# A hybrid decoder layer on one core: the output projection as seven block products per 1024 tokens

## The chip, the core and the metric

One Trainium2 chip; the program runs on one of its cores. TensorE (PE) multiplies, VectorE (DVE), ScalarE (ACT) and GpSimd (POOL) do the rest, SyncE (SP) issues the DMAs. Each engine works through its own queue in order and waits on semaphores of the others. The metric is the device time of one execution in microseconds (us); three executions of the kernel before took 2698.26 to 2699.79 us, median 2699.1.

## The reference, cut to what matters

One layer over 4096 tokens of width 1024. One input projection gives the inputs of three head groups and a gate; the branch outputs, 2048 wide together, are gated and go through one output projection, a residual add and a final norm.

```python
h = rms_norm(x, norm_g[l])
proj = h @ w_in[l]
u_lru, q_gla, k_gla, v_gla, g_lr, q_xa, gate = jnp.split(proj, split_points, axis=-1)
...                      # y_lru, y_gla, y_xa: recurrence, linear attention, cross-attention
y = jnp.concatenate([y_lru, y_gla, y_xa], axis=-1) * jax.nn.silu(gate)
x = x + y @ w_out[l]     # (4096 x 2048) @ (2048 x 1024)
...
return rms_norm(x, final_norm_g)
```

Every product of the projections is computed from operands split in two: a high part (fp32r, a rounded copy) and a low part (operand minus high part). A product is then three matmuls, high x high, high x low and low x high (`mm3`).

## The kernel before

The tokens are taken in four blocks of 1024 (BLK), each of two units of 512 (UNIT). The first stage loops over blocks, and in a block over 17 head groups, written out in `orders`: L0 to L7 (recurrence), X0 to X3 (cross-attention), V, G, Q (linear attention). For each group and unit TensorE multiplies the group's weights (whi, wlo) with the normed input (hh, hl); generators that `tick()` moves on do the rest on the other engines. Weights come through two raw buffers (L109) and are split by ScalarE (L110) and VectorE (L111). Each group's gated output, 128 channels over a block, is stored to a DRAM tile y_d (`store_y`, L297). The inputs hh, hl of a unit take 16 KB per partition each, in pool hp, two of each.

The last stage is the output projection, in 32 steps of 128 tokens. `load_y` (L754 to L763) loads the 2048 channels of 128 tokens as yr, splits them into yh (L759) and yl (L760) and loads x. `out_mm` gives, for each of the 16 channel tiles ct and the two halves n of the 1024 outputs, three matmuls of a 128 x 128 stationary piece of y and 512 columns of the weights: 96 per 128 tokens into two PSUM banks. `finish` adds the residual (L776), squares (L778), takes the root on GpSimd (`rstd_of`, L68 and L70), scales (L782, the last step L787) and stores (L783, L789). All of w_out stays in SBUF as high and low parts, split once (`wo_split`, L701 to L706): the first four channel tiles during the last head groups by `wo_gen`, into hp buffers that the first unit has left, the other twelve at the start of the stage.

What sets the order: the program is written in one order, and a scheduler then orders each engine's queue by priorities and its own estimate of time, so that instructions of neighbouring parts mix. Buffers of a pool are waited for by semaphores. PSUM has two pools of four banks, acc and aux. All DMAs go through SP's queue, in the order in which they stand there.

## Time and profile before

| | |
|---|---|
| median of three runs | 2699.1 us |
| the profiled execution: time, and its span | 2699.65 us, 2697.9 us |
| TensorE busy | 2660.9 us, 13338 matmuls |
| VectorE, ScalarE, GpSimd busy | 1381.3, 1156.6, 92.4 us |
| granted TensorE clock, mean | 0.999 |
| DMA | 231.64 MB, mean 86 GB/s |

The span is counted from the first to the last instruction that the profile shows. Matmuls are pipelined: each is drawn some 389 ns long (for 512 columns) but the next one starts while it runs, so start times give the rate and busy sums don't. In a timeline a row has its start, its length, the engine, the line of the kernel, the operation with the tile written and the tiles read, and in brackets how long the engine had been idle before and who ended that.

### The profile page before, as it was taken

The page shows a single profiled execution, that of the slowest core. Times are in us where ns is not written, and L with a number is a line of the kernel's source. Part 1 is how long each engine was busy: PE and PEld are TensorE (multiplying, and loading weights), DVE is VectorE, ACT ScalarE, POOL GpSimd, SP SyncE. Part 2 cuts the span into 40 slices and gives each one's busy share as a digit, 9 for nine tenths or more (in the row PEclk, how much of TensorE's full clock was granted, in tenths as well). Part 3 has the DMA queues.
Part 4 walks back from the last instruction along what each step waited for, and adds up shares of the span by engine and source line. Part 5 has one row for each costly group of instructions (what it writes and reads, how often), then busy time and mean ns, then how long its engine had stood idle before and what let it go on. Part 6 is the DMA issues. An engine that isn't in the chain of part 4 may idle for free.

```text
span 2697.9 us, 32855 instructions
## 1 busy us (share of the span) xinstructions
PE 2660.9 (99%) x13338; PEld 2249.6 (83%) x13338; DVE 1381.3 (51%) x2349; ACT 1156.6 (43%) x1802; POOL 92.4 (3%) x197
## 2 busy tenths in 40 slices
PE   7999999999999999999999999999999999999998
PEld 6888888888888888888887888888878888888887
DVE  6466546656664666567456757645673222222221
ACT  6355535653654465356436636643572111111110
POOL 3000000000000000000000000000000000000000
PEclk9999999999999999999999999999999999999999
DMA  8211112431212133112213312111253222222221
GB/s 276 67 59 57 63 59 71 127 99 57 67 55 75 49 119 120 58 57 65 65 49 105 116 38 82 59 61 51 65 187 131 96 102 94 94 94 94 94 94 63
DMA packets 119928, 231.64 MB, mean 86 GB/s; under 512 B 6528, under 2 KB 73184, under 8 KB 115680
## 3 DMA queue, kind: packets, MB, share of 16 engines
q1 hardware_dynamic: 119776, 229.54, 26.2%
q8 instruction: 104, 1.70, 0.3%
q14 instruction: 48, 0.39, 0.0%
HBM read 179.19 MB, written 50.33 MB: 85 GB/s over the span
## 4 chain that ended last, share of the span: by engine, by line
PE 86%; DMA 4%; DVE 4%; ACT 4%; issue 1%; POOL 1%; SPq 0%; DVEq 0%; POOLq 0%; ACTq 0%
PE out L75 8%; PE out L74 8%; PE out L76 8%; PE gate L74 7%; PE gate L75 7%; PE gate L76 7%; PE u L75 4%; PE u L76 4%; PE u L74 4%; PE q L75 3%; PE q L74 3%; PE q L76 3%; DMA x<-in_x 2%; PE vp L477 2%; PE vp L476 2%; PE vp L475 2%
## 5 line engine op out<-in xcount | busy, mean ns | idle before, releaser
L74 PE MATMUL gate<-hh,whi 128*128 128x512 f32 x1024 | 400.6, 391 | 0.0
L75 PE MATMUL out<-wolo,yh 128*128 128x512 f32 x1024 | 398.8, 389 | 0.8 <-DVE wolo L706 0.6
L76 PE MATMUL gate<-hh,wlo 128*128 128x512 f32 x1024 | 398.8, 389 | 0.0
L74 PE MATMUL out<-wohi,yh 128*128 128x512 f32 x1024 | 398.0, 389 | 0.7 <-ACT wohi L705 0.7
L75 PE MATMUL gate<-hl,whi 128*128 128x512 f32 x1024 | 398.6, 389 | 0.0
L76 PE MATMUL out<-wohi,yl 128*128 128x512 f32 x1024 | 398.4, 389 | 0.0
L111 DVE TENSOR_TENSOR wlo<-raw,whi 128x1024 fp32r<-128x1024 f32 (+2 forms) x152 | 191.4, 1281 | 216.9 <-ACT whi L110 182.5
L776 DVE TENSOR_TENSOR xr<-xr,out 128x512 f32<-128x512 f32 x64 | 43.9, 687 | 444.7 <-PE out L76 444.7
L75 PEld LDWEIGHTS out<-wolo,yh 128*128 128x128 f32 x1024 | 192.2, 188 | 42.2 <-DVE wolo L706 2.1
L74 PEld LDWEIGHTS out<-wohi,yh 128*128 128x128 f32 x1024 | 192.1, 188 | 41.0 <-ACT wohi L705 1.1
L74 PEld LDWEIGHTS gate<-hh,whi 128*128 128x128 f32 x1024 | 192.3, 188 | 40.5 <-issue 1.5
L76 PEld LDWEIGHTS gate<-hh,wlo 128*128 128x128 f32 x1024 | 192.2, 188 | 40.3
L76 PEld LDWEIGHTS out<-wohi,yl 128*128 128x128 f32 x1024 | 192.2, 188 | 39.8
L110 ACT CAST whi<-raw 128x1024 fp32r<-128x1024 f32 (+2 forms) x152 | 162.4, 1095 | 146.5 <-PE gate L75 96.1
L75 PEld LDWEIGHTS gate<-hl,whi 128*128 128x128 f32 x1024 | 192.3, 188 | 39.1
L74 PE MATMUL u<-hh,whi 128*128 128x512 f32 x512 | 203.7, 398 | 0.0
L75 PE MATMUL u<-hl,whi 128*128 128x512 f32 x512 | 199.6, 390 | 0.0
L76 PE MATMUL u<-hh,wlo 128*128 128x512 f32 x512 | 199.4, 390 | 0.0
L333 DVE SCALAR_TENSOR_TENSOR uc<-u,prm_sb,uc 128x511 f32<-128x511 f32 (+2 forms) x192 | 142.9, 745 | 67.8 <-ACT uc L330 67.3
L759 ACT CAST yh<-yr 128x2048 fp32r<-128x2048 f32 x32 | 61.2, 1912 | 257.6 <-PE out L75 256.4
L778 ACT ACTIVATE j<-xr 128x512 bf16<-128x512 f32 x64 | 40.0, 625 | 304.9 <-DVE xr L776 304.9
L74 PE MATMUL q<-hh,whi 128*128 128x512 f32 x384 | 150.3, 391 | 0.0
(219 smaller groups left out, 4976.4 us busy)
## 6 DMA issues: line engine op xcount, KB each, us to landing
raw<-in_w_oth SPq DMA_DIRECT2D x72, 512.0 KB, 3.8
raw<-in_w_lru SPq DMA_DIRECT2D x64, 576.0 KB, 3.8
yr<-y_d SPq DMA_DIRECT2D x32, 1024.0 KB, 5.2
xt<-in_x_t SPq DMA_DIRECT2D x32, 512.0 KB, 3.8
y_d<-sg SPq DMA_DIRECT2D x32, 512.0 KB, 4.0
y_d<-i SPq DMA_DIRECT2D x32, 512.0 KB, 3.2
xr<-in_x SPq DMA_DIRECT2D x32, 512.0 KB, 3.4
out<-xr SPq DMA_DIRECT2D x31, 512.0 KB, 4.1
```

The costliest lines, as they stand in the source:

```text
L74: nc.tensor.matmul(o, w_hi, r_hi, start=start, stop=False)
L75: nc.tensor.matmul(o, w_hi, r_lo, start=False, stop=False)
L76: nc.tensor.matmul(o, w_lo, r_hi, start=False, stop=stop)
L110: nc.scalar.copy(out=hi[:, i, :width], in_=raw[:, :width])
L111: nc.vector.tensor_tensor(out=lo[:, i, :width], in0=raw[:, :width], in1=hi.bitcast(F32)[:, i, :width], op=ALU.subtract)
L333: nc.vector.scalar_tensor_tensor(out=uc[:, d:UNIT], in0=o[:, 0:UNIT - d], scalar=w, in1=uc[:, d:UNIT], op0=ALU.mult, op1=ALU.add)
L475: nc.tensor.matmul(o, hh, wh, start=kt == 0, stop=False)
L476: nc.tensor.matmul(o, hh, wl, start=False, stop=False)
L477: nc.tensor.matmul(o, hl, wh, start=False, stop=kt == KT - 1)
L759: nc.scalar.copy(out=yh, in_=yr)
L776: nc.vector.tensor_tensor(out=xt[:, c], in0=xt[:, c], in1=o[n], op=ALU.add)
L778: nc.scalar.activation(out=junk, in_=xt[:, c], func=AF.Square, accum_out=ss[:, n:n + 1])
```

## The change

The output projection of a block is seen as a product of 2 x 2 blocks: w_out's 2048 x 1024 as A11, A12, A21, A22, and y's 2048 channels x 1024 tokens as B11, B12, B21, B22 (the first index is the half of the channels, the second the unit of 512 tokens). Instead of eight products of blocks it computes seven, P1 to P7, of sums and differences of blocks (Strassen's method in Winograd's form), and adds them up into the two halves of the outputs for both units.

`wout_gen`, started in the second block after its third entry, loads w_out, scales the GLA rows, makes the four sums S1 to S4 of weight blocks on VectorE and stores them, with A12 and A22, to DRAM tiles ws_d; it runs between the head groups. In the last stage nothing of w_out stays in SBUF: for each product the weights are loaded anew (`w_load`), 512 KB per step of two channel tiles, into three buffers wraw, and split into wh and wl. A product has four steps of 24 matmuls. `prep_hi` of a step is issued three steps ahead (the cast of the token side, th, and of the weights, wh), `prep_lo` two steps ahead (tl, wl). The y blocks of 2 MB each are loaded in two pieces into the four hp buffers, which the first stage now names h0 to h3; the sums of token blocks are made in place before P5 and P4. The four banks of a product are copied or added to x rows by `evac`: after P7 come the norms of the eight pieces of 128 tokens (`out_norm`), three pieces of work per step. In the last product of all, TensorE takes the four row blocks one after the other, each with its eight channel tiles, and each row block's end follows at once. y_d is laid out as 16 tiles of 128 channels x 1024 tokens.

```diff
-    y_ds = [dram.tile([NSUB, P, 16, P], F32, name=f"y_d{b}", tag=f"y_d{b}") for b in range(nblk)]
+    y_ds = [dram.tile([16, P, BLK], F32, name=f"y_d{b}", tag=f"y_d{b}") for b in range(nblk)]
+    ws_ds = [dram.tile([P, 6, 512], F32, name=f"ws_d{c}", tag=f"ws_d{c}") for c in range(8)]
...
-        hh = hp.tile([P, KT, UNIT], F32R, tag="hh", name="hh")
-        hl = hp.tile([P, KT, UNIT], F32R, tag="hl", name="hl")
+        k = hslot[0] % 2
+        hslot[0] += 1
+        hh = hp.tile([P, KT, UNIT], F32R, tag=f"h{2 * k}", name="hh")
+        hl = hp.tile([P, KT, UNIT], F32R, tag=f"h{2 * k + 1}", name="hl")
...
-        nc.sync.dma_start(out=y_ds[b][:, :, ct, :].rearrange("s p t -> p s t"),
-                          in_=y.rearrange("p (s t) -> p s t", t=P))
+        nc.sync.dma_start(out=y_ds[b][ct], in_=y)
...
+    def wout_gen():
+        for c in range(8):
+            r0 = wp.tile([P, LW], F32, tag="raw", name="raw")[:, :D]
+            r1 = wp.tile([P, LW], F32, tag="raw", name="raw")[:, :D]
+            nc.sync.dma_start(out=r0, in_=w_out[c * P:(c + 1) * P, :])
+            nc.sync.dma_start(out=r1, in_=w_out[(c + 8) * P:(c + 9) * P, :])
+            yield 1
+            yield 1
+            if c < 4:
+                nc.scalar.activation(out=r1, in_=r1, func=AF.Copy, scale=hgn[:, c:c + 1])
+            a11, a21, a12, a22 = r0[:, :512], r0[:, 512:], r1[:, :512], r1[:, 512:]
+            s1 = wk.tile([P, UNIT], F32, tag="t2", name="s1")
+            s2 = wk.tile([P, UNIT], F32, tag="t2", name="s2")
+            nc.vector.tensor_tensor(out=s1, in0=a21, in1=a22, op=ALU.add)
+            nc.vector.tensor_tensor(out=a21, in0=a11, in1=a21, op=ALU.subtract)
+            nc.vector.tensor_tensor(out=s2, in0=s1, in1=a11, op=ALU.subtract)
+            nc.vector.tensor_tensor(out=a11, in0=a12, in1=s2, op=ALU.subtract)
+            d = ws_ds[c]
+            nc.sync.dma_start(out=d[:, 0:2, :], in_=r0.rearrange("p (a n) -> p a n", a=2))
+            nc.sync.dma_start(out=d[:, 2:4, :], in_=r1.rearrange("p (a n) -> p a n", a=2))
+            nc.sync.dma_start(out=d[:, 4, :], in_=s1)
+            nc.sync.dma_start(out=d[:, 5, :], in_=s2)
...
-                if last and u == 0:
-                    spawn(pending[0] if b + 1 < nblk else wo_gen(range(0, 4)))
+                if last and u == 0 and b + 1 < nblk:
+                    spawn(pending[0])
+            if b == 1 and ei == 2:
+                spawn(wout_gen())
...
+    tsp = ctx.enter_context(tc.tile_pool(name="tsp", bufs=4))
+    wrp = ctx.enter_context(tc.tile_pool(name="wrp", bufs=3))
+    wsp = ctx.enter_context(tc.tile_pool(name="wsp", bufs=4))
+    rp = ctx.enter_context(tc.tile_pool(name="rp", bufs=1))
+    fg_b = rp.tile([P, D], F32, name="fg_b")
+    CH = 2
+    NCH = 8 // CH
+    SEQ = [("P1", None, "acc", True), ("P5", S1, "aux", True), ("P2", A12, "acc", False),
+           ("P3", S4, "aux", False), ("P6", S2, "acc", True), ("P4", A22, "aux", True),
+           ("P7", S3, "acc", False)]
+    steps = [(b, p, c) for b in range(nblk) for p in range(len(SEQ)) for c in range(NCH)]
+    B, R = {}, {}
+    place = {"B11": 2, "B22": 3, "B12": 0, "B21": 1}
+    def load_b(b, n):
+        rows = slice(0, 8) if n[1] == "1" else slice(8, 16)
+        u = int(n[2]) - 1
+        if b > 0:
+            if n == "B11":
+                place["B11"], place["B22"] = place["B22"], place["B11"]
+        t = hp.tile([P, 8, UNIT], F32, tag=f"h{place[n]}", name=n)
+        src = y_ds[b][rows, :, usl(u)].rearrange("c p t -> p c t")
+        for i in range(2):
+            nc.sync.dma_start(out=t[:, 4 * i:4 * i + 4], in_=src[:, 4 * i:4 * i + 4])
+        B[b, n] = t
...
+    T, W = {}, {}
+    def w_load(q):
+        if q >= len(steps):
+            return
+        b, p, c = steps[q]
+        raw = wrp.tile([P, CH, 512], F32, tag="wraw", name="wraw")
+        for i in range(CH):
+            ct = c * CH + i
+            slot = SEQ[p][1]
+            nc.sync.dma_start(out=raw[:, i], in_=w_out[ct * P:(ct + 1) * P, 0:512] if slot is None
+                              else ws_ds[ct][:, slot, :])
+        W[q] = raw
+    def prep_hi(q):
+        if q >= len(steps):
+            return
+        b, p, c = steps[q]
+        cs = slice(c * CH, (c + 1) * CH)
+        n = SEQ[p][0]
+        if n == "P1":
+            if c == 0 and b == 0:
+                for nm in ("B11", "B22", "B12", "B21"):
+                    load_b(b, nm)
+            t = B[b, "B11"][:, cs]
+        elif n == "P5":
+            b11, b12, b22 = (B[b, m][:, cs] for m in ("B11", "B12", "B22"))
+            t = tsp.tile([P, CH, 512], F32, tag="t1", name="t1", bufs=2)
+            nc.vector.tensor_tensor(out=t, in0=b12, in1=b11, op=ALU.subtract)
+            nc.vector.tensor_tensor(out=b12, in0=b22, in1=b12, op=ALU.subtract)
+            nc.vector.tensor_tensor(out=b11, in0=b22, in1=t, op=ALU.subtract)
+        elif n == "P2":
+            t = B[b, "B21"][:, cs]
+        elif n == "P3":
+            t = B[b, "B22"][:, cs]
+        elif n == "P6":
+            t = B[b, "B11"][:, cs]
+        elif n == "P4":
+            t = B[b, "B21"][:, cs]
+            nc.vector.tensor_tensor(out=t, in0=B[b, "B11"][:, cs], in1=t, op=ALU.subtract)
         else:
...
+            t = B[b, "B12"][:, cs]
+        th = tsp.tile([P, CH, 512], F32R, tag="th", name="th")
+        nc.scalar.copy(out=th, in_=t)
+        raw = W.pop(q)
+        wh = wsp.tile([P, CH, 512], F32R, tag="wh", name="wh")
+        nc.scalar.copy(out=wh, in_=raw)
+        T[q] = (t, th, raw, wh)
+        w_load(q + 3)
+    def prep_lo(q):
+        if q >= len(steps):
+            return
+        b, p, c = steps[q]
+        t, th, raw, wh = T[q]
+        tl = tsp.tile([P, CH, 512], F32R, tag="tl", name="tl")
+        nc.vector.tensor_tensor(out=tl, in0=t, in1=th.bitcast(F32), op=ALU.subtract)
+        wl = wsp.tile([P, CH, 512], F32R, tag="wl", name="wl")
+        nc.vector.tensor_tensor(out=wl, in0=raw, in1=wh.bitcast(F32), op=ALU.subtract)
+        T[q] = (th, tl, wh, wl)
+        if c == NCH - 1 and b + 1 < nblk:
+            for m in {"P3": ("B11",), "P4": ("B22", "B21"), "P7": ("B12",)}.get(SEQ[p][0], ()):
+                load_b(b + 1, m)
...
+    def out_norm(b, i, u):
+        r = R.pop((b, i, u))
+        ss = small.tile([P, 1], F32, tag="fss", name="fss", bufs=2)
+        junk = rp.tile([P, D], BF16, tag="j2", name="j2")
+        nc.scalar.activation(out=junk, in_=r, func=AF.Square, accum_out=ss)
+        rs = rstd_of(ss, D, 1, "f", nc.vector)
+        nc.vector.scalar_tensor_tensor(out=r, in0=r, scalar=rs, in1=fg_b, op0=ALU.mult, op1=ALU.mult)
+        tok = b * BLK + u * UNIT + i * P
+        nc.sync.dma_start(out=out[tok:tok + P, :], in_=r)
+    def evac(b, n, i, bank):
+        ra, rb = R.get((b, i, 0)), R.get((b, i, 1))
+        if n == "P1":
+            SN[i, 1] = rp.tile([P, 512], F32, tag=f"s1{i}", name="s1")
+            work.append(snap(SN[i, 1], bank))
+        elif n == "P5":
+            SN[i, 5] = rp.tile([P, 512], F32, tag=f"s5{i}", name="s5")
+            work.append(snap(SN[i, 5], bank))
+        elif n == "P2":
+            work.append(add(ra[:, H1], ra[:, H1], bank))
+        elif n == "P3":
+            work.append(add(rb[:, H1], rb[:, H1], bank))
+        elif n == "P6":
+            work.append(add(rb[:, H1], rb[:, H1], bank))
+            work.append(add(rb[:, H1], rb[:, H1], SN[i, 1]))
+        elif n == "P4":
+            work.append(add(ra[:, H2], ra[:, H2], bank, ALU.subtract))
+            work.append(add(rb[:, H2], rb[:, H2], SN[i, 5]))
+        else:
+            s1 = SN[i, 1]
+            work.append(add(s1, s1, bank))
+            work.append(add(ra[:, H2], ra[:, H2], s1))
+            work.append(lambda: out_norm(b, i, 0))
+            work.append(add(rb[:, H2], rb[:, H2], s1))
+            work.append(lambda: out_norm(b, i, 1))
     nc.sync.dma_start(out=fg_b, in_=final_g.partition_broadcast(P))
...
+    for q in range(3):
+        w_load(q)
+    for q in range(3):
+        prep_hi(q)
+        if q:
+            prep_lo(q - 1)
+    banks = {}
+    nq = len(steps)
+    for q, (b, p, c) in enumerate(steps):
+        n, _, grp, fresh = SEQ[p]
+        grp = grp if b % 2 == 0 else {"acc": "aux", "aux": "acc"}[grp]
+        if c == 0 and fresh:
+            banks[grp] = [(acc if grp == "acc" else aux)("out") for _ in range(4)]
+        if n in ("P5", "P2"):
+            load_x(b, c, 0 if n == "P5" else 1)
+        prep_hi(q + 3)
+        prep_lo(q + 2)
+        tail = q >= nq - NCH
+        if tail and c < NCH - 1:
+            pop_work(4)
+            continue
+        for i in range(4):
+            for cc in (range(NCH) if tail else [c]):
+                th, tl, wh, wl = T[q - c + cc]
+                for k in range(CH):
+                    t = slice(i * P, (i + 1) * P)
+                    st = fresh and cc == 0 and k == 0
+                    sp = cc == NCH - 1 and k == CH - 1
+                    o = banks[grp][i]
+                    sk = {} if fresh else {"skip_group_check": True}
+                    nc.tensor.matmul(o, th[:, k, t], wh[:, k], start=st, stop=False, **sk)
+                    nc.tensor.matmul(o, th[:, k, t], wl[:, k], start=False, stop=False, **sk)
+                    nc.tensor.matmul(o, tl[:, k, t], wh[:, k], start=False, stop=sp, **sk)
+            if tail:
+                evac(b, n, i, banks[grp][i])
+                pop_work(20)
+        pop_work(3)
+        if c == NCH - 1 and not tail:
+            for i in range(4):
+                evac(b, n, i, banks[grp][i])
+            if n in ("P1", "P5", "P2", "P6"):
+                pop_work(20)
+    pop_work(1000)
```

How this moves instructions, at three places.

TensorE, from the last matmul of the last gate projection (gate) on; pr and pi are the last head group's two small products, out the output projection. Before:

```order
L76 MATMUL gate<-hh,wlo 128x512
L74 MATMUL out<-wohi,yh 128x512
L75 MATMUL out<-wolo,yh 128x512
L76 MATMUL out<-wohi,yl 128x512
L74 MATMUL out<-wohi,yh 128x512
L75 MATMUL out<-wolo,yh 128x512
L76 MATMUL out<-wohi,yl 128x512
L74 MATMUL out<-wohi,yh 128x512
L75 MATMUL out<-wolo,yh 128x512
L76 MATMUL out<-wohi,yl 128x512
L74 MATMUL out<-wohi,yh 128x512
L74 MATMUL pr<-uhi,whi 128x512
```

and with the change:

```order
L77 MATMUL gate<-hh,wlo 128x512
L75 MATMUL pr<-uhi,whi 128x512
L75 MATMUL pi<-uhi,whi 128x512
L76 MATMUL pr<-ulo,whi 128x512
L77 MATMUL pr<-uhi,wlo 128x512
L76 MATMUL pi<-ulo,whi 128x512
L77 MATMUL pi<-uhi,wlo 128x512
L943 MATMUL out<-wh,th 128x512 x2
L944 MATMUL out<-wl,th 128x512
L945 MATMUL out<-wh,tl 128x512
L943 MATMUL out<-wh,th 128x512
```

Ten matmuls of the output projection stood ahead of pr and pi and more between them; now all six of pr and pi come first, and the new stage behind them.

VectorE, the output projection away from its ends. Before, this is what it has for 128 tokens (split of y, sum of squares, scaling, two residual additions), then the next:

```order
L760 TENSOR_TENSOR yl<-yr,yh 128x2048
L779 TENSOR_TENSOR fss<-fss 128x1
L782 SCALAR_TENSOR_TENSOR xr<-xr,fr,fg_b 128x1024
L776 TENSOR_TENSOR xr<-xr,out 128x512 x2
L760 TENSOR_TENSOR yl<-yr,yh 128x2048
```

With the change, at the end of what is left of the first block (r is a piece of x with its sums, fm and fr belong to its norm) while the second block's P5 is prepared (t, and B_16881 and B_17337, are token sums; tl and wl the low parts of the third and fourth step of P5):

```order
L868 TENSOR_TENSOR r<-r,s_16514 128x512
L824 TENSOR_TENSOR B_17337<-B_17188,B_17337 128x1024
L69 TENSOR_SCALAR fm<-fss 128x1
L825 TENSOR_TENSOR B_16881<-B_17188,t_17693 128x1024
L882 SCALAR_TENSOR_TENSOR r<-r,fr,fg_b 128x1024
L69 TENSOR_SCALAR fm<-fss 128x1
L851 TENSOR_TENSOR tl<-t_17589,th 128x1024
L882 SCALAR_TENSOR_TENSOR r<-r,fr,fg_b 128x1024
L853 TENSOR_TENSOR wl<-wraw,wh 128x1024
L851 TENSOR_TENSOR tl<-t_17693,th 128x1024
L853 TENSOR_TENSOR wl<-wraw,wh 128x1024
```

The low parts of these two steps stand behind the last scalings of the block before and behind the token sums of the fourth step.

VectorE, the last rows of the program. Before:

```order
L776 TENSOR_TENSOR xr<-xr,out 128x512 x2
L779 TENSOR_TENSOR fss<-fss 128x1
L782 SCALAR_TENSOR_TENSOR xr<-xr,fr,fg_b 128x1024
L776 TENSOR_TENSOR xr<-xr,out 128x512 x2
L779 TENSOR_TENSOR fss<-fss 128x1
L787 SCALAR_TENSOR_TENSOR xr<-xr,fr,fg_b 128x512 x2
```

and with the change (the last two of four row blocks):

```order
L868 TENSOR_TENSOR r<-r,s_19977 128x512 x2
L69 TENSOR_SCALAR fm<-fss 128x1
L882 SCALAR_TENSOR_TENSOR r<-r,fr,fg_b 128x1024
L69 TENSOR_SCALAR fm<-fss 128x1
L882 SCALAR_TENSOR_TENSOR r<-r,fr,fg_b 128x1024
L868 TENSOR_TENSOR s_19978<-s_19978,out 128x512
L868 TENSOR_TENSOR r<-r,s_19978 128x512 x2
L69 TENSOR_SCALAR fm<-fss 128x1
L882 SCALAR_TENSOR_TENSOR r<-r,fr,fg_b 128x1024
L69 TENSOR_SCALAR fm<-fss 128x1
L882 SCALAR_TENSOR_TENSOR r<-r,fr,fg_b 128x1024
```

The last scalings were of one piece of 128 tokens, in two halves; now each row block ends with two pieces of 128 x 1024, whose small step and scaling stand one behind the other ahead of the next row block's additions.

## Rows read from the trace of the kernel before

**Rows 1.** The page: busy times; the chain that ended last, by engine

```profile
PE 2660.9 (99%) x13338; PEld 2249.6 (83%) x13338; DVE 1381.3 (51%) x2349; ACT 1156.6 (43%) x1802; POOL 92.4 (3%) x197
...
PE 86%; DMA 4%; DVE 4%; ACT 4%; issue 1%; POOL 1%; SPq 0%; DVEq 0%; POOLq 0%; ACTq 0%
```

**Rows 2.** Instructions that write tile out: count, ns least/median/most, first and last start

```profile
L74 PE MATMUL out<-wohi,yh x1024: 388/389/497, 1989.6 to 2690.0; 128*128 128x512 f32 x171
...
L76 PE MATMUL out<-wohi,yl x1024: 388/389/397, 1990.1 to 2690.5; 128*128 128x512 f32 x171
```

**Rows 3.** Stretches: length, busy PE, PEld, DVE, ACT, POOL, clock, DMA, GB/s

```profile
1980.00:2000.00 20.00, 19.80 (x88) 15.96 (x87) 14.58 (x24) 17.42 (x24) 0.00 (x0) 1.00 0.35 116
2000.00:2020.00 20.00, 19.17 (x82) 14.90 (x81) 13.89 (x16) 13.36 (x16) 0.00 (x0) 1.00 0.90 304
2020.00:2060.00 40.00, 39.36 (x173) 32.04 (x172) 17.46 (x18) 12.05 (x18) 1.48 (x4) 1.00 0.41 145
```

**Rows 4.** Timeline of TensorE: start us, length us, line, instruction

```profile
1989.42 0.39 PE L76 MATMUL gate<-hh,wlo 128*128 128x512 f32 x1
...
1992.27 0.50 PE L74 MATMUL pr<-uhi,whi 128*128 128x512 f32 x1 [0.20 <-ACT uhi L339]
...
1993.80 0.40 PE L76 MATMUL pi<-uhi,wlo 128*128 128x512 f32 x1
```

**Rows 5.** Timeline of the DMA queue SP, same stretch

```profile
1995.51 1.42 SPq L795 DMA_DIRECT2D wraw<-in_w_out  x3
```

**Rows 6.** Timeline of the scalar engine, same stretch

```profile
1993.64 0.72 ACT L365 ACTIVATE a<-r,c4n 128x512 f32<-128x512 f32 x1 [1.42 <-DVE r L362]
...
2001.01 0.62 ACT L361 ACTIVATE a<-a 128x512 f32<-128x512 f32 x1
```

**Rows 7.** Groups of instructions by line and shape: busy us, mean ns, idle before

```profile
L111 DVE TENSOR_TENSOR wlo<-raw,whi 128x1024 fp32r<-128x1024 f32 x80 | 95.7, 1222 | 85.9 <-ACT whi L110 51.5 <-PE pT L434 34.1
...
L110 ACT CAST whi<-raw 128x1024 fp32r<-128x1024 f32 x80 | 81.3, 1049 | 60.0 <-PE gate L75 40.6 <-PE k L75 18.7 <-DMA raw<-in_w_mem 0.6
...
L776 DVE TENSOR_TENSOR xr<-xr,out 128x512 f32<-128x512 f32 x64 | 43.9, 687 | 444.7 <-PE out L76 444.7
...
L782 DVE SCALAR_TENSOR_TENSOR xr<-xr,fr,fg_b 128x1024 f32<-128x1024 f32 x31 | 39.8, 1285 | 29.1 <-POOL fr L70 29.1
```

**Rows 8.** DMA issues by line: engine, count, KB each, median us to landing

```profile
yr<-y_d SPq DMA_DIRECT2D x32, 1024.0 KB, 5.2
...
out<-xr SPq DMA_DIRECT2D x31, 512.0 KB, 4.1
...
wraw<-in_w_out SPq DMA_DIRECT2D x12, 512.0 KB, 5.4
```

**Rows 9.** Timeline of TensorE near the start of the run

```profile
46.50 0.52 PE L475 MATMUL vp<-whi,hh 128*128 128x272 f32 x2 [1.46 <-ACT whi L110]
```

**Rows 10.** Busy by engine in three stretches right there

```profile
46.00:48.00 2.00, 1.35 (x7) 0.93 (x8) 2.00 (x4) 2.00 (x4) 0.00 (x0) 1.00 0.98 398
48.00:50.00 2.00, 2.00 (x10) 2.00 (x11) 2.00 (x4) 1.58 (x4) 0.00 (x0) 0.55 0.69 205
50.00:52.00 2.00, 2.00 (x12) 2.00 (x12) 0.27 (x1) 1.15 (x2) 0.21 (x2) 0.60 0.79 260
```

**Rows 11.** Timeline of the vector engine: two instructions of 1024 back to back

```profile
1969.83 2.36 DVE L706 TENSOR_TENSOR wolo<-raw,wohi 128x1024 fp32r<-128x1024 f32 x2
```

**Rows 12.** Timeline of all engines at the end of the run

```profile
2690.91 0.69 DVE L776 TENSOR_TENSOR xr<-xr,out 128x512 f32<-128x512 f32 x1 [10.19 <-PE out L76]
...
2693.54 1.42 DVE L787 SCALAR_TENSOR_TENSOR xr<-xr,fr,fg_b 128x512 f32<-128x512 f32 x2 [0.94 <-POOL fr L70]
2694.32 1.00 SPq L789 DMA_DIRECT2D out<-xr  x2
```

**Rows 13.** Timeline of the DMA queue SP in the second block

```profile
652.88 1.48 SPq L109 DMA_DIRECT2D raw<-in_w_lru  x2
```

**Rows 14.** Timeline of the scalar engine in the second block

```profile
675.06 2.20 ACT L110 CAST whi<-raw 128x1152 fp32r<-128x1152 f32 x2
```

More of the change, by code (lines that the diff above doesn't have):

```diff
@@ L693, in hybrid_layer @@
     load_next(1)
[L696 to L715 removed]
+    S4, S3, A12, A22, S1, S2 = range(6)
+    def wout_gen():
[20 more added lines that the diff above has]
+            nc.sync.dma_start(out=d[:, 5, :], in_=s2)
+            yield 1
             yield 1
@@ new lines, in load_x @@
+    def load_x(b, i, u):
+        t = rp.tile([P, D], F32, tag="r", name="r", bufs=8)
+        tok = b * BLK + u * UNIT + i * P
+        nc.sync.dma_start(out=t, in_=x[tok:tok + P, :])
+        R[b, i, u] = t
+    T, W = {}, {}
[10 more added lines that the diff above has]
+        W[q] = raw
@@ new lines, in hybrid_layer, with pop_work, add, snap @@
+    work = []
+    def pop_work(n):
+        for _ in range(n):
+            if work:
+                work.pop(0)()
+    def add(o, i0, i1, op=ALU.add):
+        return lambda: nc.vector.tensor_tensor(out=o, in0=i0, in1=i1, op=op)
+    def snap(o, i):
+        return lambda: nc.scalar.copy(out=o, in_=i)
+    H1, H2 = slice(0, 512), slice(512, 1024)
+    SN = {}
+    def out_norm(b, i, u):
[5 more added lines that the diff above has]
+        nc.vector.scalar_tensor_tensor(out=r, in0=r, scalar=rs, in1=fg_b, op0=ALU.mult, op1=ALU.mult)
+        tok = b * BLK + u * UNIT + i * P
+        nc.sync.dma_start(out=out[tok:tok + P, :], in_=r)
```

88 lines of the change are left out of this document (2 added, 86 removed).

## The prediction

> **What bounds the kernel now.** I read the page's busy table and its chain first. TensorE is busy for 2660.9 us of 2697.9 us, and the chain that ended last runs through TensorE for 86% of the span [rows 1]. So time can only be won where TensorE gets less to do, and is lost wherever it waits. The change is in the last stage, so I asked next for the tile "out": its matmuls start at 1989.6 us and the last one at 2690.5 us, three groups of 1024 [rows 2]. A busy figure says nothing about their rate, since each is drawn 389 ns long and they overlap. I take the rate from first and last start: 700.9 us from 1989.6 to 2690.5, less 1.7 us in which TensorE stood idle early in the stage (80 us less 19.80, 19.17 and 39.36 [rows 3]), less twelve matmuls of the last head group that lie between them (12 x 0.227 = 2.7 us). That leaves 696.5 us for 3072, or 0.2267 us each. The stage is one unbroken run of matmuls at full clock; vector, scalar and DMA work lie under it.
>
> **What goes.** Per 1024 tokens there were 8 token blocks x 2 halves x 16 x 3 = 768 matmuls; now there are 7 products x 4 row blocks x 8 x 3 = 672, of the same shape. Over four blocks 384 are gone: 384 x 0.2267 = 87.1 us. The waits come more often (two per 24 matmuls). A wait that is already satisfied shows no gap in the run above, so I price it at nothing; if each of the 224 cost 0.2 us it would be 45 us, which is a rival below.
>
> **The seam between the stages.** This is the first place shown in the order of TensorE. Before, the last gate matmul starts at 1989.42, and ten out matmuls of head start are queued behind it, with operands split long ago; they bridge the time until the last head group's pr arrives at 1992.27; that group's last pi matmul starts at 1993.80 [rows 4]. Now nothing of the out stage stands before pr and pi, because its first weights are loaded late: their buffers come free with those last matmuls (the load of wraw is issued at 1995.51 [rows 5], right behind two other loads), and their cast stands on the scalar engine behind that head group's activations. Four pieces follow.
> - TensorE has nothing between the slot after the gate, 1989.65, and 1992.27: 2.6 us. The six matmuls then take it to 1993.85.
> - The scalar engine's run from 1993.64 to the end of the one at 2001.01 (2001.5) [rows 6] has the same eleven instructions now and one more 512-wide activation, about 0.5 us (half of the 1.05 us cast [rows 7], an estimate). So the first weight cast runs from 2002.05 to 2003.1, and the first out matmul starts then: 9.3 us idle. The load itself, issued by 1994.2 and 5.4 us long [rows 8], would be there by about 2000, so it doesn't end last.
> - The second kind of matmul waits for the low part, 1.22 us on the vector engine [rows 7], of which two matmuls hide 0.8: 0.4 us. The fourth step's low part stands in the vector queue behind six sums of token blocks, which wait for loads of 1 MB (5.2 us each [rows 8]) issued near 2002.5; walking the queue I get it 0.7 us late.
> - After 9 us of idleness I expect the clock at the lower of its two levels (1.2 rather than 2.4 GHz). Early in this run, behind a wait of 1.46 us [rows 9], the granted clock fell to 0.55 and 0.60 in two following stretches of 2 us [rows 10]: 0.45 x 2 + 0.40 x 2 = 1.7 us of full speed lost.
>
> Together 2.6 + 9.3 + 0.4 + 0.7 + 1.7 = 14.7 us, less the 1.7 us idle that the old seam had: +13.0 us. Below it could be 8 us (if the scheduler's scalar order binds less and the load does), above it 20 us (if the 5.5 MB asked for at the seam delay the second and third step).
>
> **Inside a block.** A step of 24 matmuls lasts 24 x 0.2267 = 5.44 us, a block 152.4 us. The vector engine has per block 56 low parts, 12 + 4 token sums of 1024 at 1.222 us, 36 additions of 512 at 0.687 us, 8 scalings at 1.285 us [rows 7] and 8 small ones, 1.3 us together: 88.0 + 24.7 + 10.3 + 1.3 = 124.3 us, 82% of the block. The scalar engine has 56 casts at 1.049, and 8 snapshots of 512 and 8 squares of 1024 that I price like casts of their size: near 73 us (an estimate). Both fit on average. But the work isn't even. In the first two products of blocks 2, 3 and 4, the vector queue holds the rest of the block before (12 additions, 8 scalings, 8 small), and the sums of P5. From the end of P7 TensorE has six steps and two matmuls (33.1 us) before it needs the low part of the third step of P5. Ahead of that in the queue (second place in the order) stand 12 additions, 8 small, 8 scalings and 14 of 1024: 8.2 + 1.3 + 10.3 + 17.1 = 36.9 us by whole durations, so 3.8 us late. But two 1024-wide ones back to back take 2.36 us [rows 11], not 2.45: each next starts 0.08 us before the end; 42 x 0.08 = 3.4 us less gives 33.5 us, 0.4 us late. The Trainium skill ("VectorE: DVE Perf Modes", The DRAIN you can't avoid) holds that the next operation doesn't start until the pipe has emptied, unless nothing holds it. By that rule the sum would be 0.8 us worse at each border than what I take, and by the spacing 2.6 us better; the row shows the shorter spacing for two that don't depend on each other, and about half of the 42 do depend on the one before. I take 3.0 us per border, near the longer sum, since a scaling also waits for GpSimd; 3 x 3.0 = +9 us, with ends of 0.5 and 6 us per border (1.5 to 18).
>
> Weights, token blocks, x and out move 30 MiB per block now, 31.5 MB / 155 us = 203 GB/s; the trace reached 398 GB/s over a short stretch [rows 10]. The three weight buffers turn round in three steps (16.3 us): a load of 5.4 us, cast and low part take 7.7 us. That leaves room, and I price it at nothing; above, it is the slower rival.
>
> **The end.** Before, the last addition starts at 2690.91, the scaling at 2693.54, its store is issued at 2694.32 and the span ends at 2697.9 [rows 12], 7.0 us after the last matmul. Now each row block of 128 has two token halves behind it (third place in the order). From the last addition to the scaling it was 2.63 us; one more addition stands in front (0.7), the square goes over 1024 rather than 512 (0.5 more, half a cast), and the small step is on the vector engine rather than on GpSimd (0.3 less, an estimate): the first scaling starts 2.63 + 0.7 + 0.5 - 0.3 = 3.5 us after the bank. It takes 1.29 us, then small step, GpSimd hop and second scaling take another 2.1 us: 6.9 us of the vector engine per row block, while TensorE brings one every 5.44 us. Over three of them 4.3 us pile up. The last store is issued 4.3 + 6.9 + 0.3 = 11.5 us after the last matmul and lands 4.1 us later [rows 8]: 15.6 us, +8.6. I take +9 us (5 to 12).
>
> **The weight sums, in the second block of the projections.** 32 additions of 0.687 us and four scalar passes, with 16 loads and 32 stores, are spread over eight head groups of about 24 us (some 108 matmuls). The stores hold the two raw buffers, so SP waits and the next group's weights load later. Before, such a load is issued at 652.88 [rows 13] and cast at 675.06 [rows 14], some 20 us after it landed, which is what hides it. A cast a few us late would hold the scalar queue, but TensorE then still has projections into four banks. I take +2 us (0 to 12). The store of y in longer pieces changes nothing on the path.
>
> **Sum.** -87.1 + 13.0 + 9 + 9 + 2 = -54.1 us. The profiled execution took 2699.65 us, so 2645.5 us; the median of the runs is 0.55 us lower: 2645 us.
>
> **Rivals.** (1) Better: the vector queue overlaps at borders as its spacing says, the seam costs 8 us, the end 7: -87.1 + 8 + 1.5 + 7 = -71 us, 2628 us. For it: all ends are measured on waits that other orders may hide. Against: the scalar order at the seam is fixed. 12%. (2) Worse at borders: in the strict queue each of the eight scalings stands 0.9 us for GpSimd, as the last one before did [rows 12], unfilled: 7.2 + 3.8 = 11 us per border, 33 us; with 20 at the seam and 11 elsewhere -87 + 64 = -23 us, 2676 us. For it: 82% load with no slack at these places. Against: other vector work stands between small step and scaling nearly everywhere. 21%. (3) The waits at the steps cost 0.2 us each: 45 us, -9 us, 2690 us. Against: no such gap in the old stage. 4%. (4) Slower: the ring of three weight buffers becomes the bound. SP is one queue, and a weight load stands behind stores and x loads that wait for stores (4.1 us); if a turn takes over 16.3 us, each of 112 steps is a third of the excess longer. The gain of 54 us is gone at 0.48 us per step, a turn of 17.8 us: a load would have to take 15.5 us instead of 5.4. With a turn of 19 us: 112 x 0.9 = 101 us, +47 us, 2746 us. 4%. My forecast: 59%.
>
> **Numbers.** About 0.2% (5 us) is what a measurement of this kernel can tell from no change. Faster 0.95, within 0.01, slower 0.04. The range of 8 in 10 reaches from rival 1 over the forecast to rival 2: 2627 to 2680 us.
>
> **What would show it.** Right: 2688 out matmuls at 0.227 us; one gap of about 9 us on TensorE before the first of them, released by the cast of wh on the scalar engine, with a clock near half behind it; at three borders a gap of 1 to 6 us, released by wl on the vector engine in P5; some 15 us from the last matmul to the end. Wrong: gaps at every step (the ring or the waits), a spacing above 0.23 us, or waits for whi in the second block of the projections of more than 10 us in all.

## The result, and the profile after

The changed kernel takes 2637.4 us (median of four runs, 2636.0 to 2639.9) where the kernel before took 2699.4 us in the same session: a ratio of 0.977 with a 95% interval of 0.9753 to 0.9787. 62 us are gone; 54 were forecast. The profiled execution took 2638.2 us, its span is 2636.1 us, so I compare it with the span of 2697.9 us of before: -61.8 us.

First the page: busy us, share of the span and instructions of each engine, and the chain that ended last. They answer to [rows 1].

```profile
PE 2581.3 (98%) x12954; PEld 2182.4 (83%) x12954; DVE 1686.8 (64%) x2700; ACT 1316.5 (50%) x1950; POOL 92.1 (3%) x165
...
PE 82%; DVE 9%; DMA 3%; ACT 3%; issue 2%; POOL 1%; SPq 0%; POOLq 0%; DVEq 0%; ACTq 0%
```

TensorE is still the bound, but the vector engine now has 9% of the chain, up from 4%. Where TensorE waited in the last stage stands in its waits from 1990 to 2640 us (line, releaser, us in all, times, longest):

```profile
PE out L943 <- ACT wh L841: 6.8, 1, 6.8
PE out L944 <- DVE wl L853: 5.8, 3, 1.9
PE pr L76 <- DVE ulo L344: 1.0, 1, 1.0
```

In the order of these rows: one hole at the seam, three at the borders of the blocks, and one ahead of the stage, within the last head group; no wait is drawn at the other steps. The matmuls that write the tile "out" (count, ns, first and last start) answer to [rows 2]:

```profile
L943 PE MATMUL out<-wh,th x896: 388/389/796, 1998.8 to 2620.6; 128*128 128x512 f32 x180
...
L945 PE MATMUL out<-wh,tl x896: 388/389/632, 2000.7 to 2621.1; 128*128 128x512 f32 x180
```

3 x 896 = 2688 of them, 384 fewer. Single ones now last up to 796 ns: some ran at the lower clock. The seam in TensorE's timeline (start, length, line, instruction, in brackets the idle time before and its releaser) answers to [rows 4]:

```profile
1988.56 0.39 PE L77 MATMUL gate<-hh,wlo 128*128 128x512 f32 x1
1989.02 0.50 PE L75 MATMUL pr<-uhi,whi 128*128 128x512 f32 x1
...
1990.77 0.50 PE L76 MATMUL pr<-ulo,whi 128*128 128x512 f32 x1 [1.02 <-DVE ulo L344]
...
1991.57 0.40 PE L77 MATMUL pi<-uhi,wlo 128*128 128x512 f32 x1
1998.77 1.22 PE L943 MATMUL out<-wh,th 128*128 128x512 f32 x2 [6.80 <-ACT wh L841]
```

The scalar engine there, to be laid beside [rows 6]:

```profile
1988.94 0.72 ACT L369 ACTIVATE a<-r,c4n 128x512 f32<-128x512 f32 x1
...
1997.16 0.62 ACT L365 ACTIVATE a<-a 128x512 f32<-128x512 f32 x1
1997.68 1.03 ACT L841 CAST wh<-wraw 128x1024 fp32r<-128x1024 f32 x1
```

The cast of wh follows the activations without a pause, so the weights were there, if only just (their loads are issued from 1992.06 on); r8 below, where they come much earlier, shows that it is the scalar queue that sets the start. The clock behind the hole and behind the first border, in stretches of 2 us (columns as in [rows 3]):

```profile
1998.00:2000.00 2.00, 1.22 (x2) 0.50 (x2) 2.00 (x3) 1.77 (x3) 0.00 (x0) 0.50 0.95 320
...
2004.00:2006.00 2.00, 2.00 (x7) 1.54 (x7) 0.26 (x1) 0.63 (x1) 0.00 (x0) 0.67 1.04 395
...
2188.00:2190.00 2.00, 0.56 (x2) 0.46 (x3) 2.00 (x3) 0.18 (x1) 0.00 (x0) 0.91 0.64 221
2190.00:2192.00 2.00, 2.00 (x6) 1.56 (x5) 2.00 (x3) 0.00 (x0) 0.00 (x0) 0.50 0.65 192
2192.00:2194.00 2.00, 2.00 (x8) 1.62 (x7) 2.00 (x3) 0.68 (x1) 0.00 (x0) 0.74 1.00 378
```

A granted clock of 0.50 is the lower of the two levels (1.2 of 2.4 GHz). Before each fall TensorE had stood idle: 6.8 us at the seam, 1.9 us at the border. The vector engine at the first border, from its first addition behind P7 on; TensorE waits for the last of these rows:

```profile
2152.90 1.28 DVE L868 TENSOR_TENSOR s<-s,out 128x512 f32<-128x512 f32 x2
...
2185.32 1.21 DVE L851 TENSOR_TENSOR tl<-t,th 128x1024 fp32r<-128x1024 f32 x1
2186.97 1.29 DVE L882 SCALAR_TENSOR_TENSOR r<-r,fr,fg_b 128x1024 f32<-128x1024 f32 x1 [0.44 <-POOL fr L71]
2188.17 1.22 DVE L853 TENSOR_TENSOR wl<-wraw,wh 128x1024 fp32r<-128x1024 f32 x1
```

And the end, where the first additions behind the second and the last row block and the last scaling answer to [rows 12]:

```profile
2611.98 0.68 DVE L868 TENSOR_TENSOR s<-s,out 128x512 f32<-128x512 f32 x1
...
2625.64 0.68 DVE L868 TENSOR_TENSOR s<-s,out 128x512 f32<-128x512 f32 x1
...
2631.27 1.28 DVE L882 SCALAR_TENSOR_TENSOR r<-r,fr,fg_b 128x1024 f32<-128x1024 f32 x1 [0.72 <-POOL fr L71]
```

Two row blocks take 13.66 us of the vector engine, 6.83 each, while TensorE brings one in 5.44 us. The last addition starts 4.3 us after the last matmul's slot (2621.1 + 0.23).

### The profile page after: what moved, and what is told of

The parts are those of the page before. It is cut to its first block, busy times and chain, and to the rows that moved or that the text cites. A ratio compares the mean times of both kernels' runs of the same rounds, so it can differ in the third digit from the quotient of the medians.

```text
span 2636.1 us, 33203 instructions
## 1 busy us (share of the span) xinstructions
PE 2581.3 (98%) x12954; PEld 2182.4 (83%) x12954; DVE 1686.8 (64%) x2700; ACT 1316.5 (50%) x1950; POOL 92.1 (3%) x165
## 3 DMA queue, kind: packets, MB, share of 16 engines
q1 hardware_dynamic: 111440, 300.86, 33.5%
## 4 chain that ended last, share of the span: by engine, by line
PE 82%; DVE 9%; DMA 3%; ACT 3%; issue 2%; POOL 1%; SPq 0%; POOLq 0%; DVEq 0%; ACTq 0%
PE gate L75 8%; PE gate L77 8%; PE gate L76 8%; PE out L944 6%; PE out L945 6%; PE out L943 6%; PE u L77 4%; PE u L76 4%; PE u L75 4%; PE q L76 3%; PE q L75 3%; PE q L77 3%; PE vp L481 2%; PE vp L479 2%; PE vp L480 2%
## 5 line engine op out<-in xcount | busy, mean ns | idle before, releaser
L943 PE MATMUL out<-wh,th 128*128 128x512 f32 x896 | 351.0, 392 | 6.8 <-ACT wh L841 6.8
L944 PE MATMUL out<-wl,th 128*128 128x512 f32 x896 | 351.4, 392 | 5.9 <-DVE wl L853 5.8
L945 PE MATMUL out<-wh,tl 128*128 128x512 f32 x896 | 350.9, 392 | 0.0
L838 ACT CAST th<-B 128x1024 fp32r<-128x1024 f32 x96 | 101.1, 1053 | 281.3 <-PE out L944 281.3
L851 DVE TENSOR_TENSOR tl<-B,th 128x1024 fp32r<-128x1024 f32 x96 | 117.5, 1224 | 144.6 <-ACT th L838 143.9
L944 PEld LDWEIGHTS out<-wl,th 128*128 128x128 f32 x896 | 169.7, 189 | 43.4 <-DVE wl L853 7.9
L943 PEld LDWEIGHTS out<-wh,th 128*128 128x128 f32 x896 | 169.6, 189 | 42.4 <-ACT wh L841 7.2
L945 PEld LDWEIGHTS out<-wh,tl 128*128 128x128 f32 x896 | 169.6, 189 | 35.3
L296 DVE SCALAR_TENSOR_TENSOR sg<-sg,gate 128x512 f32<-128x512 f32 x128 | 86.7, 683 | 105.7 <-ACT sg L295 105.4
L295 ACT ACTIVATE sg<-gate 128x512 f32<-128x512 f32 x128 | 75.9, 600 | 152.4 <-PE gate L77 148.0
```

Of the source, the lines that this page charges most:

```text
L296: nc.vector.scalar_tensor_tensor(out=sg[:, usl(u)], in0=sg[:, usl(u)], scalar=1.0, in1=g, op0=ALU.add, op1=ALU.mult)
L838: nc.scalar.copy(out=th, in_=t)
L851: nc.vector.tensor_tensor(out=tl, in0=t, in1=th.bitcast(F32), op=ALU.subtract)
L943: nc.tensor.matmul(o, th[:, k, t], wh[:, k], start=st, stop=False, **sk)
L944: nc.tensor.matmul(o, th[:, k, t], wl[:, k], start=False, stop=False, **sk)
L945: nc.tensor.matmul(o, tl[:, k, t], wh[:, k], start=False, stop=sp, **sk)
```

## The experiments

All ratios are to the kernel before. Differences of a few microseconds lie inside the intervals of two such ratios, so each verdict rests on the trace, and the medians only have to agree. The kernel before stood beside each group of runs: 2699.0 us for r1 to r4, 2699.5 for r5 to r8, 2701.4 for r9 and r10. Where a run is set against r1 from another group, the difference by the ratios is given too.

**r1, the changed kernel once more.** 

> The changed kernel itself, beside the three that follow, so that a few microseconds can be compared on one chip. All theories: 2634 to 2640 us (its runs were 2636.0 to 2639.9).

2638.2 us, ratio 0.9771 (0.9757 to 0.9784). Holes of 6.8, 1.9, 1.9 and 1.9 us as before; the out stage lasts 620.5 us from first to last start. In the profile above it was 622.3: there the clock fell behind two of the three borders, here, with the same kernel, behind the third alone (0.84, 0.50 and 0.81 in its three stretches). This is what r2 to r10 are compared with.

**r2, first weights early.** The pool wrp lies in front of tsp in memory (t1 goes to wsp for room), and the first casts and low parts are put ahead in their queues:

```diff
+    wrp = ctx.enter_context(tc.tile_pool(name="wrp", bufs=3))
     tsp = ctx.enter_context(tc.tile_pool(name="tsp", bufs=4))
-    wrp = ctx.enter_context(tc.tile_pool(name="wrp", bufs=3))
...
-        nc.scalar.copy(out=wh, in_=raw)
+        with (tc.high_priority() if q < 3 else ExitStack()):
+            nc.scalar.copy(out=wh, in_=raw)
...
-        nc.vector.tensor_tensor(out=wl, in0=raw, in1=wh.bitcast(F32), op=ALU.subtract)
+        with (tc.high_priority() if q < 3 else ExitStack()):
+            nc.vector.tensor_tensor(out=wl, in0=raw, in1=wh.bitcast(F32), op=ALU.subtract)
```

> The three weight buffers lie where the projections stop reading earlier, and the first three casts and low parts of w_out go ahead of the last activations of the head groups. Theory A (the 6.8 us hole at the seam is the cast of wh standing behind the activations on the scalar engine, and the slow matmuls behind it come from that hole): the hole falls from 6.8 us to 1 us or less, the matmuls at 0.43 us behind it go too, and the time falls by 6 to 9 us, to about 2629. Theory B (the first weights themselves arrive late, or the token blocks do): the hole stays within 1 us of 6.8, and the time within 2 us. Where the three casts only push the head groups' activations back and these are waited for, a new hole of up to 3 us would show in the last pr and pi.

2631.2 us, 0.9746 (0.9733 to 0.9759): -7.0 us. Its waits in the last stage:

```profile
PE out L946 <- DVE wl L855: 5.8, 3, 1.9
PE out L945 <- ACT wh L842: 1.2, 1, 1.2
```

The hole fell from 6.8 to 1.2 us and the borders stayed. The slow matmuls behind it were to go too, and they didn't (columns as in [rows 3]):

```profile
1996.00:1998.00 2.00, 2.00 (x6) 1.61 (x6) 2.00 (x2) 1.97 (x3) 0.00 (x0) 0.50 1.05 389
```

With 0.81 and 0.83 in the stretches beside it, 1.7 us of full speed are lost. So theory A holds for the hole and misses on the clock. The edit also brings the first loads forward (from 1992.06 to 1959.23), so by itself it doesn't tell theory A from B; r8 does.

**r3, scalings later.**

```diff
+    norms = []
...
-            work.append(lambda: out_norm(b, i, 0))
             work.append(add(rb[:, H2], rb[:, H2], s1))
-            work.append(lambda: out_norm(b, i, 1))
+            late = b + 1 < nblk
+            (norms if late else work).insert(i if late else len(work), lambda: out_norm(b, i, 0))
+            (norms if late else work).append(lambda: out_norm(b, i, 1))
...
         pop_work(3)
+        if b > 0 and p < 2:
+            norms.pop(0)()
```

> In blocks 2 to 4 the eight scalings of the block before are issued one per step of the first two products instead of all in the first, so about five of them stand behind the low part of P5's third step. Same instructions, other order. Theory A (vector queue too long ahead of that low part): the three holes of 1.9 us and the slow matmuls behind them go, the time falls by 6 to 10 us, to about 2629. Theory B (the weights' load or cast is late there): the holes stay, time within 2 us. Theory C (vector engine short on average over the block): the holes only move a few steps on, time within 3 us.

2630.3 us, 0.974 (0.9726 to 0.9753): -7.9 us. Its waits in the last stage, whole:

```profile
PE out L945 <- ACT wh L841: 6.8, 1, 6.8
PE pr L76 <- DVE ulo L344: 1.0, 1, 1.0
```

All three border holes are gone, with the same instructions in another order; the out stage is 611.9 us long, 8.6 less. Theory A holds; B and C fall.

**r4, a shorter end.**

In out_norm the norm's small step goes to GpSimd in the last block, the steps of the last product take six pieces of work each instead of four, and in evac:

```diff
             work.append(add(rb[:, H2], rb[:, H2], SN[i, 5]))
+            if b == nblk - 1:
+                work.append(add(ra[:, H2], ra[:, H2], SN[i, 1]))
+                work.append(add(rb[:, H2], rb[:, H2], SN[i, 1]))
...
+        elif b == nblk - 1:
+            work.append(add(ra[:, H2], ra[:, H2], bank))
+            work.append(lambda: out_norm(b, i, 0))
+            work.append(add(rb[:, H2], rb[:, H2], bank))
+            work.append(lambda: out_norm(b, i, 1))
```

> In the last block alone the sums with P1's snapshot are made before the last product, so two additions instead of three follow each bank, and the small step of the norm runs on GpSimd. Vector work per row block behind the last product falls from 6.8 us to about 5.5 us, against 5.4 us of TensorE. Theory A (the end is the pile-up of three row blocks, 3 x 1.4 = 4.2 us, and one chain of 6.8 us): from the last matmul to the end falls from 15.0 us to about 10 us, time -4 to -5.5 us, about 2632. Theory B (the end is the last row block's own chain only, no pile-up): -1.3 us. Theory C (the stores set the end): within 1 us of no change.

2633.9 us, 0.9756 (0.9743 to 0.977): -4.4 us. The vector engine at its end:

```profile
2610.06 1.28 DVE L868 TENSOR_TENSOR r<-r,out 128x512 f32<-128x512 f32 x2
2612.93 1.28 DVE L882 SCALAR_TENSOR_TENSOR r<-r,fr,fg_b 128x1024 f32<-128x1024 f32 x1 [1.60 <-POOL fr L71]
...
2616.14 1.28 DVE L868 TENSOR_TENSOR r<-r,out 128x512 f32<-128x512 f32 x2
```

A row block takes 6.08 us, not the 5.5 I expected: the first scaling waits 1.60 us, for the square on the scalar engine and then for both small steps on GpSimd. From the last matmul's start to the end it is 12.0 us where it was 15.0, so 3.0 us less: four times the 0.75 us saved per row block, as a pile-up gives; the last chain alone would give 0.75. So theory A is right in kind, and its end of about 10 us was too short. The other 1.4 us of the median don't come from the end: in the two profiles the stage itself begins 1.2 us earlier (1999.2, in r1 2000.4), ahead of anything that this edit touches.

**r5, no weight sums.** The generator isn't started, and each product reads a plain block of w_out.

```diff
-            if b == 1 and ei == 2:
-                spawn(wout_gen())
...
-            nc.sync.dma_start(out=raw[:, i], in_=w_out[ct * P:(ct + 1) * P, 0:512] if slot is None
-                              else ws_ds[ct][:, slot, :])
+            nc.sync.dma_start(out=raw[:, i], in_=w_out[ct * P:(ct + 1) * P, 0:512])
```

> The generator that makes and stores the six sums of weight blocks is left out, and every product streams a plain block of w_out (so the output isn't the layer's); the last stage moves and computes as much as before. Theory A (the sums cost what their vector and DMA work pushes back in the second block of the projections: predicted 2 us, 2.6 us by the trace of the changed kernel, 488.9 us from the first vp of block 2 to that of block 3 where the kernel before has 486.3): the second block falls back to about 486.3 us, time -2 to -4 us, about 2635. Theory B (the sums are free; the 2.6 us are the scatter between builds): within 1 us of no change in that block.

2634.9 us, 0.9757 (0.9743 to 0.9772): -3.3 us, -3.8 by the ratios. The first vp of block 2 and of block 3, in the kernel before, the changed kernel and this one:

```profile
530.21 0.37 PE L475 MATMUL vp<-whi,hh 128*128 128x272 f32 x1
...
1016.48 0.37 PE L475 MATMUL vp<-whi,hh 128*128 128x272 f32 x1
```

```profile
528.25 0.37 PE L479 MATMUL vp<-whi,hh 128*128 128x272 f32 x1
...
1017.11 0.37 PE L479 MATMUL vp<-whi,hh 128*128 128x272 f32 x1
```

```profile
529.23 0.37 PE L479 MATMUL vp<-whi,hh 128*128 128x272 f32 x1
...
1014.28 0.37 PE L479 MATMUL vp<-whi,hh 128*128 128x272 f32 x1
```

The block takes 486.3, 488.9 and 485.1 us: the sums cost 2.6 us against the kernel before and 3.8 us against this one. Theory A holds: in nine of the ten profiles with the sums the block takes 488.8 to 489.7 us. The size is known no better than that, since an edit elsewhere shifts this block too: in r3, which changes only the last stage, it took 492.3 us. Which part of the sums costs it, vector work, loads or stores, isn't shown.

**r6 and r7, the same extra vector work in two places.** Behind the low parts of P5 (r6) or P3 (r7):

```diff
+        if b > 0 and SEQ[p][0] == "P5":
+            for _ in range(2):
+                nc.vector.scalar_tensor_tensor(out=t, in0=t, scalar=0.0, in1=t, op0=ALU.mult, op1=ALU.add)
```

> Two vector instructions of 1.28 us that change nothing are added to each step of product P5 in blocks 2 to 4, 24 in all (30 us of vector work). Theory A (what counts is the queue ahead of the low part of P5's third step, which four of them join): the three holes grow by 3 to 5 us each from 1.9 us (part of it fills the six waits of 0.43 us for GpSimd), time +9 to +16 us, about 2651. Theory B (what counts is the vector engine's share over the block, 124 of 152 us, which stays under 100% with 10 us more): within 2 us of no change. Theory C (the engine has no slack anywhere): +30 us.

> The same 24 vector instructions, in product P3 of the same blocks, where little else stands in the vector queue. Theory A: no new hole, holes at P5 unchanged at 1.9 us, time within 2 us of 2638. Theory B: the same. Theory C: +30 us, as in P5.

In P5 2649.8 us, 0.9814 (0.98 to 0.9829): +11.5 us on r1, +11.6 by the ratios. In P3 2636.7 us, 0.9768 (0.9753 to 0.9782): -1.5 us, -0.8 by the ratios, no change. The waits for the vector engine with the work in P5, then in P3:

```profile
PE out L947 <- DVE wl L853: 9.9, 3, 3.3
...
PE out L946 <- DVE fm L69: 2.5, 2, 1.3
PE out L946 <- DVE s L871: 1.3, 1, 1.3
```

```profile
PE out L947 <- DVE wl L853: 5.8, 3, 1.9
```

In P5 the holes at the third step grew by 1.4 us each, less than the 3 to 5 us of theory A, but each border got a second hole of 1.3 us, and the rest is slow clock behind them: the out stage is 632.0 us long, 11.5 more. So A is right in place and total, not in how the loss is divided. That 30 us of vector work cost 11.5 us here and nothing there rules out B and C.

**r8, two weight buffers.** The load also moves from prep_hi into prep_lo, behind the low part.

```diff
-    wrp = ctx.enter_context(tc.tile_pool(name="wrp", bufs=3))
+    wrp = ctx.enter_context(tc.tile_pool(name="wrp", bufs=2))
...
-        w_load(q + 3)
+        w_load(q + 2)
```

> Two weight buffers in place of three; a load is issued when the low part of the step two before it is made. By the forecast's figures a turn has two steps, 10.9 us, for load 5.4 + cast and low part 2.3 = 7.7 us and the time until its buffer comes free. Theory A (three buffers have room, two just about): no change or some holes, 0 to +15 us. Theory B (rival 4 of the forecast: the ring is near its limit already): a hole at most of the 112 steps, 1 to 3 us each, +100 us or more.

2637.4 us, 0.977 (0.9754 to 0.9787): -0.8 us, -0.3 by the ratios, no change, and one new wait of 0.39 us, at the seam. The ring has a whole buffer to spare; rival 4 was far off.

This run also settles theory B of r2. Here the first two buffers are loaded far ahead of the seam (the DMA queue), and the hole is the same (TensorE's wait):

```profile
1819.63 1.28 SPq L805 DMA_DIRECT2D wraw<-in_w_out  x3
```

```profile
PE out L943 <- ACT wh L841: 6.8, 1, 6.8
```

The first matmul starts at 1999.13, so its weights were asked for 179 us before, and it starts no sooner behind the last gate matmul than in the changed kernel (10.2 us in both). The arrival of the weights doesn't set the start.

**r9, r2 + r3 + r4 together.** 

> The three edits of r2, r3 and r4 together. If the seam, the borders and the end are separate terms of one sum, their gains add: 7.0 + 7.9 + 4.4 = 19.3 us, about 2619. If two of them pay with the same slack (the vector queue), less: 2622 to 2628.

2619.7 us, 0.9699 (0.9686 to 0.9713): the gains add (18.5 us of 19.3, 19.4 by the ratios). This beats both kernels. Of the waits of the out matmuls 1.2 us at the seam and one of 0.3 us are left. The matmuls of its last stage:

```profile
L954 PE MATMUL out<-wh,th x896: 388/389/499, 1993.1 to 2602.7; 128*128 128x512 f32 x180
...
L956 PE MATMUL out<-wh,tl x896: 388/389/398, 1994.7 to 2603.2; 128*128 128x512 f32 x180
```

2687 spacings in 610.1 us, less 0.4 us at the one hole inside it, are 0.2269 us each: with the holes closed the stage is matmuls at the old rate and nothing else.

**r10, more scalar work at the seam.**

```diff
+        with (tc.high_priority() if q < 4 else ExitStack()):
+            for _ in range(2 if q < 4 else 1):
+                nc.scalar.copy(out=th, in_=t)
```

> Each of the first four casts of token blocks is made twice and goes ahead, so that 4.2 us more of scalar work (4 x 1.05) stand before the cast of wh at the seam; the kernel before had 7.9 us of such casts there, the changed one 4.2. Theory A (the seam came out 3.9 us shorter than forecast because this work left the scalar queue, which the forecast had kept in its start time): the first matmul of the last stage starts 3 to 4.5 us later against the last gate matmul (10.2 us behind it in the changed kernel), time +3 to +5 us, about 2642. Theory B (the arrival of the weights sets the start): 10.2 us as before, time within 1 us.

2640.5 us, 0.9781 (0.9768 to 0.9794): +2.3 us (+2.7 by the ratios), a little under the range. In its trace:

```profile
1990.94 0.39 PE L77 MATMUL gate<-hh,wlo 128*128 128x512 f32 x1
...
2004.23 2.07 PE L945 MATMUL out<-wh,th 128*128 128x512 f32 x4 [10.91 <-ACT wh L843]
```

The stage starts 13.3 us after the last gate matmul, not 10.2: +3.1 us for 4.2 us of casts. Theory A holds, with a part of the casts still hidden; B falls, since the weights' loads came no later (issued 2.5 us behind the last gate matmul, in the changed kernel 3.5).

## Why the prediction was right

It was right in kind and nearly in size. From the start of the last gate matmul to that of the last out matmul before had 701.1 us (1989.4 to 2690.5, [rows 2, 4]), after has 632.5 (1988.6 to 2621.1): -68.5. The matmuls are -87.1 of it, the borders +9.6 by their gaps and clock (below), so the seam is what is left. Term by term, in us:

| term | forecast | measured | shown by |
|---|---|---|---|
| 384 matmuls | -87.1 | -87.1 | r9: 0.2269 us each |
| seam | +13.0 | +9.0 | r2: -7.0, r8, r10 |
| three borders | +9 | +9.6 | r3: -7.9 |
| end | +9 | +7.6 | r4: -4.4 |
| weight sums | +2 | +2.6 | r5: -3.3 |
| rest of the projections | 0 | -3.5 | not explained |
| sum | -54.1 | -61.8 | span: -61.8 |

**The matmuls.** The rate of 0.2267 us was right, the waits at the steps cost nothing (rival 3), and the ring had room (rival 4, r8). But two slips cancel in the rate's working. Between the first and the last out start of before lie six matmuls of the last head group, not twelve: the six of pr and pi, from 1992.27 on [rows 4]. And TensorE lost 3.1 us there from start to start, not 1.7. The trace shows these two as the largest holes:

```profile
2003.23 1.20 PE L74 MATMUL out<-wohi,yh 128*128 128x512 f32 x4 [0.65 <-ACT wohi L705]
...
2029.84 0.50 PE L75 MATMUL out<-wolo,yh 128*128 128x512 f32 x1 [0.64 <-DVE wolo L706]
```

The starts before them are at 2002.20 and 2028.81, 1.03 us earlier each, so 0.8 us are lost at each, not 0.65: a matmul drawn 389 ns long where the next could follow after 227 hides up to 0.16 us of a hole. The old seam's own loss in the next term is 3.1 us by the same count.

**The seam** is the step that failed: the term that was mis-sized. I took the scalar engine's run of [rows 6] as it stood, from 1993.64 on, and put the cast of wh behind it at 2002.05. It came at 1997.68. What the change takes out of this queue ahead of that run stands in the trace of before, with the cast of u (uhi) just ahead of the run:

```profile
1964.48 1.91 ACT L759 CAST yh<-yr 128x2048 fp32r<-128x2048 f32 x1 [0.28 <-DMA yr<-y_d]
...
1967.92 1.99 ACT L705 CAST wohi<-raw 128x1024 fp32r<-128x1024 f32 x2
...
1976.62 1.04 ACT L705 CAST wohi<-raw 128x1024 fp32r<-128x1024 f32 x1
...
1979.27 1.04 ACT L705 CAST wohi<-raw 128x1024 fp32r<-128x1024 f32 x1
...
1981.36 1.90 ACT L759 CAST yh<-yr 128x2048 fp32r<-128x2048 f32 x1
...
1991.60 0.62 ACT L339 CAST uhi<-uc 128x512 fp32r<-128x512 f32 x1 [1.05 <-DVE uc L335]
```

The first five are 7.9 us of casts; the change has four casts of 1.04 us there instead. So the run began at 1988.94, right behind uhi and 0.4 us behind the start of the last gate matmul, where it had been 4.2 us, and pr waited less as well (1.6 us lost around it, not 2.6). I had counted what the change adds behind the seam, but not what it takes away ahead of it. r10 gave back 4.2 us of such casts and got 3.1 us of delay.

The scalar queue isn't alone in this. Just ahead of the run of before the scalar engine stood 1.05 us for uc and 1.42 us for r [rows 6], both on the vector engine, which had been busy with hardly a gap since this low part of y:

```profile
1983.29 2.29 DVE L760 TENSOR_TENSOR yl<-yr,yh 128x2048 fp32r<-128x2048 f32 x1 [0.94 <-ACT yh L759]
```

The change has low parts of 1.22 us there instead, and this one had itself waited for one of the casts (yh). How the 3.8 us between 4.2 and 0.4 divide between the two queues isn't shown.

The other pieces, from start to start: behind the first matmul TensorE lost 3.4 us where I had 0.4 + 0.7 + 1.7. Of these 0.5 is the wait for the low part wl; the fourth step had no wait; and the low clock, 0.50 from the first matmul to 2004 and 0.67 in the next 2 us, cost the other 2.9, more than the 1.7 that I took from [rows 10]. The old seam's loss to be taken off was 3.1, not 1.7. Together 1.6 + 7.0 + 3.4 - 3.1 = 8.9 us, which agrees with the 9.0 of the table.

**The borders.** The place (P5's third step), the releaser (wl on the vector engine) and the queue ahead of it were as forecast. I took 3.0 us each; TensorE loses 2.1 us from start to start, and behind two of the three 1.7 us more at the lower clock, which the forecast hadn't counted: 3 x 2.1 + 2 x 1.7. So the total is right partly by luck, and in r1 the clock fell behind one border only. Whole durations would have made it 3.8 us late and the spacing 0.4. The queue took 36.5 us, from the first addition at 2152.90 to the end of wl at 2189.39: the 33.5 of the spacing and 2.6 more because six of the eight scalings waited some 0.43 us for GpSimd, which leaves 0.4. But it began 1.4 us before the end of P7 (2154.29), on row blocks of P7 that were done, which the forecast hadn't counted: 36.5 - 1.4 - 33.1 = 2.0 us. By the rule of the Trainium skill ("VectorE: DVE Perf Modes", The DRAIN you can't avoid) it would have been the 3.8 us of whole durations; the trace agrees with the exception, for instructions that nothing holds: from wl at 2188.17 to the next, at 2189.31, it is 1.14 us for a duration of 1.22. Where an instruction reads what the one before it wrote there is no such gain: from the addition at 2611.98 to the next it is 0.72 us for a duration of 0.68.

**The end.** Forecast: 6.9 us of vector work per row block, 4.3 us of pile-up, 15.6 us from the last matmul to the end. Measured: 6.83, 4.3 and 14.8. The store landed in 3.5 us, not 4.1.

**The projections.** The sums cost about what I priced. The rest, -3.5 us (-2.0 up to block 2, -1.3 in block 3, -0.2 in block 4), is in code that the change leaves alone. TensorE's first waits, for GpSimd, were 11.9 us before and 9.6 after, and they differ between profiles of the changed kernel too (10.7 in r1); the third block took 486.8 us before and 485.4 to 486.4 in the changed kernel and its variants. Why isn't shown.
